# Position steps of a Fourier layer: turning tiles in halves of 64 rows, and where two splits stand

## The chip, the core and the metric

The kernel runs on one core of one Trainium2 chip. The metric is the device time of one execution in microseconds. The core has a matrix engine (TensorE, PE; its weight loads are shown as PEld), three engines for elementwise work (VectorE, DVE; ScalarE, ACT; GpSimd, POOL) and a queue engine (SyncE, SP). Each takes its instructions in a fixed order and waits on semaphores. Matmuls accumulate in PSUM, eight banks of 512 floats on each of 128 partitions; everything else lies in SBUF.

## The reference

Two layers over 2048 prompt rows and 512 sample rows of width 1024, in float32. The first is windowed attention; the change does not touch it. The second mixes by a two-dimensional Fourier transform over positions and over the channels of each of four groups, gates the result, projects it, adds the residual, and a last norm follows:

```python
def fourier_layer(x, g, w_gate, w_out):
    b, s, d = x.shape
    h = rmsnorm(x, g)
    hg = h.astype(jnp.float32).reshape(b, s, N_FGROUPS, FGROUP_CH)
    f = jnp.fft.fftn(hg, axes=(1, 3), norm="ortho").real
    f = f.reshape(b, s, d).astype(x.dtype)
    gate = h @ w_gate
    return x + (f * jax.nn.silu(gate)) @ w_out
...
return rmsnorm(x, final_norm)
```

## The kernel before

Float32 products are made of three matmuls: each operand is split into a high part, rounded to the matmul's input type (a cast on ScalarE), and a low part, the rest (a subtraction on VectorE), and `matmul3` (L91 to L94) adds high by high, high by low and low by high. So each operand costs one instruction on ScalarE and one on VectorE, and each block of a product three on TensorE.

The Fourier layer first transforms over channels, then over positions. The 2048 prompt positions are taken as 16 x 128: a radix-16 step by additions gives, for each of the frequencies k1 = 0 to 8, a real and an imaginary state (`gr`, `gs`, 128 x 1024), and `position` (L1363) multiplies these by cosine and sine tables. It works in two halves of 512 columns. For each half `halves_of` (L1349) splits the state, cosine products go into one bank (`A`), sine products into half of another (`B`), and from them four short VectorE instructions (L1391 to L1394) make rows of one or two tiles, `u` and its mirror (k1 and 16 - k1). Each tile is then multiplied by its gate, which was stored in DRAM as `s2d` (L1397).

A finished tile (128 positions x 1024 channels) is multiplied by the output weights `wo`. For that it has to be turned, channels onto partitions: eight transposes of 128 x 128 for a tile, four to a bank, on TensorE against an identity, then casts and subtractions out of PSUM into the two parts. The rows of a mirrored tile stand backwards, and are read backwards out of PSUM.

There are two ways from there.

- For the early frequencies (`step`, L1584, called from `emit` for 0 and 8, then 4, then 2), `split_T` (L993) turns each tile, and `finish` (L1417) multiplies it by all of `wo`, 24 matmuls of 512 columns into each of two banks `fo`, adds the residual, squares, takes the norm and writes the rows out. While TensorE works on these products, VectorE makes the states of the odd frequencies (L1706 to L1720).
- For frequencies 6, 1, 7, 3 and 5, `Outs` (L1430) takes both tiles of a pair together, and replaces the eight block products of the pair by seven (a Strassen scheme with sums of weights `T1`, `T2`, `T3`, `N4`, which were made earlier and stored). `operands` (L1470) turns the two tiles into four banks `tr` (L1442), makes the parts of the blocks themselves (`own`, L1446: cast L1449, subtraction L1450) and the sums of blocks `F1` to `F4` (`sums`, L1453: L1459, L1466) with their parts `S1` to `S4` (`split`, L986: cast L988, subtraction L990). `products` (L1483) issues seven products of twelve matmuls each into three banks `Wo`, `Zo`, `Xo`, and adds them to the residual tiles `xa`, `xb` (L1490).

The products of one pair and the position step of the next are interleaved by hand: `products` takes three hooks, and the loop at L1743 passes in `split_g` (loads and the first half's split), `transform` (the position step) and `turns` (operands of the next pair). In the steady steps TensorE thus does 84 matmuls of 512 columns, 12 of 260 (cosines), 12 of 256 (sines) and 16 transposes for each pair.

Within each engine a scheduler orders the instructions, from priorities in the order of recording and from dependences. `after(a, b)` (L134) pins one instruction behind another on its engine without a wait, and `seq(engine, ins)` (L139) pins it behind the last one that was given for the same key. The attention layer pins its long chains so; the Fourier layer pins only two sorts of instruction: the final scaling of a tile behind the last short instruction of a position step (`last_b`), and a few in the first products.

PSUM in this layer: three banks for the products (`psum2`), and five single banks in rotation (`psum3`, L1258) for the transposes and for `A` and `B`, all handed out by `bank` (L76). `left`, `right`, `xtile` and the tag `hT` (8 buffers) are pools of SBUF.

Of the kernel before, what the change touches and what calls it, by code (L numbers as in the profile page):

```python
# [9 lines left out]
F32 = mybir.dt.float32  # L10
# [9 lines left out]
P = 128  # L20
# [22 lines left out]
def encoder(  # L43
# [32 lines left out]
    def bank(name):  # L76
        return banks[-1].tile([P, 512], F32, tag="bank", name=name)

# [12 lines left out]
    def matmul3(out, a, b, start, stop, more=False):  # L91

        for i, j in ((0, 0), (0, 1), (1, 0)):
            pe(PE.matmul(out, a[i], b[j], start=start and i + j == 0, stop=stop and i == 1, skip_group_check=more))  # L94
# [871 lines left out]
    def fourier_phase(tail):  # L966
        with ExitStack() as es:
# [18 lines left out]
            def split(t, src, lo_engine=DVE):  # L986

                ACT.copy(t[:, 0], src)  # L988
                for cs in (slice(0, 256), slice(256, 512)) if lo_engine is POOL else (slice(0, 512),):
                    lo_engine.tensor_tensor(t[:, 1, cs], src[:, cs], f32(t[:, 0, cs]), ALU.subtract)  # L990
                return t[:, 0], t[:, 1]
# [20 lines left out]
            def sumsq(src, name, place=lambda ins: None):  # L1012
                ss = main.tile([P, 8], F32, tag="ss", bufs=2, name=f"ss{name}")
                junk = fp.tile([P, 512], F32, tag="c12", bufs=1, name=f"jk{name}").bitcast(BF16)
                ACT.activation(junk, src, AF.Square, accum_out=ss[:, 0:1])
                return inv_rms(ss, 1, f"inv{name}", place)
# [10 lines left out]
            class Pair:  # L1027
# [37 lines left out]
                def sums(self, i):  # L1065
# [4 lines left out]
                    if i % 2:  # L1070
# [3 lines left out]
                        2: lambda: (F[1], ps[0, 0], ALU.subtract),  # L1074
                        3: lambda: (ps[0, 0], out, ALU.subtract),
                        4: lambda: (ps[0, 1], F[2], ALU.subtract),
# [47 lines left out]
            def prod(out, a, b, ks, first):  # L1124

                for k in ks:
                    cs = slice(k * P, (k + 1) * P)
                    matmul3(out, (a[0][:, cs], a[1][:, cs]), b[k], first and k == 0, k == 3, not first)
# [129 lines left out]
            banks.append(es.enter_context(tc.tile_pool(name="psum3", bufs=5, space=PSUM, reuse_waits="tile")))  # L1258
# [76 lines left out]
            def gated(name, r, place):  # L1335
# [3 lines left out]
                if r[2] is None:  # L1339
                    SP.dma_start(s2, rows(src, (r[0] - off, r[1])))  # L1340
# [8 lines left out]
            def halves_of(name, gr, gs, hf):  # L1349

                out = []
                for i, g in enumerate((gr, gs)):
                    if g is not None:
# [3 lines left out]
                        DVE.tensor_tensor(t[:, 1], gv, f32(t[:, 0]), ALU.subtract)  # L1357
# [3 lines left out]
            last_b = [None]  # L1361

            def position(name, tab, gr, gs, tiles, loads=None, parts=None, between=None, later=None):  # L1363
# [3 lines left out]
                bp = bank(f"B{name}")  # L1367
                us = [zt(f"u{name}_{i}") for i in range(len(tiles))]
                for hf in range(2):
# [4 lines left out]
                    def acc(out, tabs, c0, n):  # L1374
                        for i, (w, t) in enumerate(zip(tabs, ts)):
# [4 lines left out]
                            matmul3(out, w, v, i == 0, i == len(ts) - 1)  # L1380

                    a = bank(f"A{name}_{hf}")[:, :260].rearrange("p (g c) -> p g c", g=2)
                    acc(a, (cs, ns), 0, 130)
                    b = bp[:, hf * 256 : hf * 256 + 256].rearrange("p (g c) -> p g c", g=2)
                    acc(b, (sn, cs), P, P)
# [9 lines left out]
                for u, s2 in zip(us, s2s):  # L1395
                    if later is None:
                        DVE.tensor_tensor(u, u, s2, ALU.mult)  # L1397
# [7 lines left out]

            def normed(x2, r):

                inv = sumsq(x2, f"f{r[0]}")
                after(DVE.scalar_tensor_tensor(x2, x2, inv[:, 0:1], gfb, ALU.mult, ALU.mult), last_b[0])
                SP.dma_start(out_rows(r), x2)  # L1410
# [6 lines left out]
            def finish(uT, r):  # L1417
                r0 = r[0]
                x2 = residual(r)
                for half in range(2):  # L1420
                    ps = psum2.tile([P, 512], F32, tag="acc", name=f"fo{r0}_{half}")
                    for k in range(KD):
                        matmul3(ps, uT[k], wo[half * KD + k], k == 0, k == KD - 1)
                    xs = x2[:, half * 512 : half * 512 + 512]
                    DVE.tensor_tensor(xs, xs, ps, ALU.add)
                normed(x2, r)
# [3 lines left out]
            class Outs:  # L1430
# [6 lines left out]
                def turn(self, i, hf):  # L1437
                    u, r = self.us[i]
                    ps = bank(f"tr{self.n}_{i}{hf}")
                    for k in range(4):  # L1440
                        c0 = (hf * 4 + k) * P
# [427 lines left out]
```

## Time and profile before

| what | value |
|---|---|
| time, median of 3 runs | 1581.89 us (1580.86 to 1582.9) |
| time of the profiled execution | 1581.36 us |
| its span, first to last instruction | 1579.4 us |
| granted TensorE clock, mean | 0.999 |
| ScalarE busy | 876.9 us (56%) |
| GpSimd busy | 446.1 us (28%) |
| HBM traffic | 236 GB/s over the span |

In rows of the profile a time stands first (us from the span's start), then a duration, the engine, the line of the kernel, the operation, output tile `<-` inputs with the numbers of buffers left out, the shapes, and how many such instructions in a row the line stands for. Matmuls overlap in the engine, so their durations (0.39 us for one of 512 columns) are longer than the distance between two of them. In brackets stands how long the engine had been idle before, and what ended that. "PEld" rows are the loads of the stationary operand, which can run under the matmul before.

### The profile page before, as it was taken

How to read it: one execution, taken by the hardware profiler on the slowest of the kernel's cores; microseconds unless marked ns; L12 is line 12 of the kernel's file. 1: busy time of each engine (PE TensorE's matmuls, PEld its weight loads, DVE VectorE, ACT ScalarE, POOL GpSimd, SP SyncE). 2: the span in 40 equal slices, each digit the busy share in tenths (PEclk: the TensorE clock that was granted, in tenths of full speed). 3: DMA queues.
4: the chain of work that ended last, by engine and by line, in shares of the span. 5: the costliest groups of instructions: out<-in, count | busy, mean ns of one | idle time of the engine just before them, and what ended most of it. 6: DMA issues, size and time to landing. Idle time of an engine off the chain costs nothing.

```text
span 1579.4 us, 27487 instructions
## 1 busy us (share of the span) xinstructions
PE 1569.1 (99%) x9754; PEld 1321.5 (84%) x9754; DVE 1152.7 (73%) x2793; ACT 876.9 (56%) x2096; POOL 446.1 (28%) x614
## 2 busy tenths in 40 slices
PE   9999999999999999999999999999999999999998
PEld 7888888888888888988888888888888888888886
DVE  6888656877547786378764577669878877989796
ACT  7788535776246784167752476646655554343242
POOL 2575642421404314024222242223112111010110
PEclk9999999999999999999999999999999999999999
DMA  8587695575856567665649556675557569557762
GB/s 302 200 332 283 226 360 210 207 257 202 295 209 222 204 235 272 223 208 220 257 161 334 211 212 227 246 251 204 203 202 259 177 219 407 181 182 299 280 208 80
DMA packets 100996, 373.89 MB, mean 237 GB/s; under 512 B 11267, under 2 KB 22283, under 8 KB 83452
## 3 DMA queue, kind: packets, MB, share of 16 engines
q1 hardware_dynamic: 83148, 298.17, 53.4%
q0 software_dynamic: 16400, 70.04, 11.5%
q10 hardware_dynamic: 1312, 3.94, 0.6%
q8 instruction: 77, 1.26, 0.3%
q14 instruction: 59, 0.48, 0.1%
HBM read 280.84 MB, written 91.26 MB: 236 GB/s over the span
## 4 chain that ended last, share of the span: by engine, by line
PE 95%; DVE 3%; DMA 1%; ACT 1%; issue 1%; POOL 0%; SPq 0%; POOLq 0%; ACTq 0%; DVEq 0%
PE gp L94 14%; PE qp L94 14%; PE spt L94 11%; PE op L94 7%; PE av L590 6%; PE W L94 6%; PE spt L505 6%; PE fo L94 5%; PE vp L94 3%; PE Wo L94 3%; PE Z L94 3%; PE pt L564 3%; PE z L94 2%; PE Zo L94 2%; PE X L94 2%; PE z L1112 1%
## 5 line engine op out<-in xcount | busy, mean ns | idle before, releaser
L94 PE MATMUL gp<-h,wg 128*128 128x512 f32 x960 | 237.8, 396 | 0.0
L94 PE MATMUL qp<-h,wq 128*128 128x512 f32 x960 | 236.9, 395 | 0.0
L524 DVE CUSTOM_DVE_ANT_0 S<-spt,b 128x385 f32<-128x385 f32 (+1 forms) x320 | 156.5, 527 | 105.2 <-PE spt L505 68.0
L94 PEld LDWEIGHTS gp<-h,wg 128*128 128x128 f32 x960 | 174.9, 188 | 37.3 <-issue 1.0
L94 PEld LDWEIGHTS qp<-h,wq 128*128 128x128 f32 x960 | 174.9, 188 | 36.3 <-issue 0.2
L532 ACT ACTIVATE S<-S 128x385 f32<-128x385 f32 (+1 forms) x320 | 188.8, 597 | 19.6 <-DVE S L524 19.3
L572 ACT CAST pts<-pt 128x384 fp32r<-128x384 f32 (+1 forms) x240 | 100.4, 458 | 165.6 <-PE pt L564 156.3
L573 DVE TENSOR_TENSOR pts<-pt,pts 128x384 fp32r<-128x384 f32 (+1 forms) x240 | 114.2, 519 | 23.9 <-ACT pts L572 22.9
L94 PE MATMUL spt<-wo,uT 128*128 128x512 f32 x480 | 120.4, 391 | 0.0
L614 POOL TENSOR_TENSOR uT<-o,uT 128x256 fp32r<-128x256 f32 x75 | 55.5, 740 | 229.6 <-ACT uT L613 224.9
L94 PE MATMUL op<-wo,uT 128*128 128x512 f32 x480 | 118.9, 391 | 0.0
L505 PE MATMUL spt<-kwin,qab 64*128 64x384 f32 (+1 forms) x960 | 118.9, 353 | 0.0
L590 PEld LDWEIGHTS av<-pts,v 128*128 128x128 f32 x576 | 101.4, 188 | 18.8
L94 PE MATMUL fo<-wo,tTu 128*128 128x512 f32 x480 | 115.8, 392 | 0.2 <-ACT wo L1624 0.2
L590 PE MATMUL av<-pts,v 128*128 128x512 f32 (+1 forms) x576 | 115.7, 341 | 0.0
L94 PEld LDWEIGHTS op<-wo,uT 128*128 128x128 f32 x480 | 89.3, 188 | 18.6
L94 PEld LDWEIGHTS spt<-wo,uT 128*128 128x128 f32 x480 | 89.1, 188 | 18.3
L94 PEld LDWEIGHTS fo<-wo,tTu 128*128 128x128 f32 x480 | 88.2, 188 | 17.5 <-ACT wo L1624 0.6
L544 DVE TENSOR_SCALAR S<-S 128x384 f32<-128x384 f32 (+1 forms) x192 | 95.8, 499 | 6.8
L505 PEld LDWEIGHTS spt<-kwin,qab 64*128 64x128 f32 x960 | 74.7, 186 | 28.3 <-issue 26.1
L610 POOL TENSOR_TENSOR o<-o,s 128x256 f32<-128x256 f32 x75 | 55.3, 737 | 134.9 <-DVE o L608 134.5
L564 PEld LDWEIGHTS pt<-ident,S 64*128 64x128 f32 x1328 | 78.4, 138 | 4.2 <-issue 2.1
(333 smaller groups left out, 3195.5 us busy)
## 6 DMA issues: line engine op xcount, KB each, us to landing
wo<-wsd SPq DMA_DIRECT2D x32, 1024.0 KB, 5.2
wq<-wsd SPq DMA_DIRECT2D x31, 1024.0 KB, 7.3
wg<-wsd SPq DMA_DIRECT2D x31, 1024.0 KB, 5.6
x<-x1d SPq DMA_DIRECT2D x40, 512.0 KB, 3.6
b<-b21d SPq DMA_DIRECT2D x40, 512.0 KB, 5.8
b<-rowd SPq DMA_DIRECT2D x40, 384.0 KB, 4.3
xs<-in_x_dram SPq DMA_DIRECT2D x23, 512.0 KB, 6.9
s2d<-gt POOLq DMA_DIRECT2D x40, 256.0 KB, 5.0
```

Source lines behind the costliest of these rows:

```text
L94: pe(PE.matmul(out, a[i], b[j], start=start and i + j == 0, stop=stop and i == 1, skip_group_check=more))
L505: pe(PE.matmul(banks[j][:, 2 + k0 * P : 2 + k1 * P], res["q"][rows, qp, b * P : (b + 1) * P], kwin[g][rows, kp, b * P + k0 * P : b * P + k ...
L524: seq(DVE, DVE.tensor_tensor_reduce(out=s[:, e0:e1], in0=ps[:, 1 + e0 : 1 + e1], in1=st["bias"][:, j, 386 - e1 : 386 - e0][:, ::-1], scale ...
L532: last_exp[0] = seq(ACT, ACT.activation(s[:, e0:e1], s[:, e0:e1], AF.Exp, bias=s[:, 386:387], scale=-1.0, accum_out=s[:, 387:388]))
L544: seq(DVE, DVE.tensor_scalar(s[:, ks], s[:, ks], den, None, ALU.mult))
L564: pe(PE.transpose(ps[h][:, kb, j, :], ss[j][rows, 1 + kb * P : 1 + (kb + 1) * P], ident[rows, rows]))
L572: seq(ACT, ACT.copy(hi, ps[:, k0:k1]))
L573: seq(DVE, DVE.tensor_tensor(lo, ps[:, k0:k1], f32(hi), ALU.subtract))
L590: pe(PE.matmul(to, v, pt, start=n == part == 0, stop=part == 1 and n in (1, len(todo) - 1), skip_group_check=n > 1,))
L610: eng.tensor_tensor(o, o, s, ALU.mult)
L614: low = eng.tensor_tensor(lo, o, f32(hi), ALU.subtract)
L1112: PE.matmul(to, m[part][:, g * P : (g + 1) * P], ch[:, 0, :, odd * P : (odd + 1) * P], start=part == 0, stop=part == 1,)
```

## The change

- **Turning.** From frequency 4 on, a tile is turned by 16 transposes of 64 rows x 128 columns in place of 8 of 128 x 128. The upper and the lower 64 rows go to two neighbouring banks, alternating (`half_turns`). Both tiles of a pair are turned one directly after the other, and pinned behind the matmuls that stand ahead of them. Whoever reads a turned block then reads pieces of 64, in turn from the two banks (`quarters`).
- **Banks.** The five single banks are given up after frequencies 0 and 8; in their place come two pairs of banks (`psum4`). Cosine and sine products of a half share one pair, and a turned tile takes one pair, so the two pairs rotate: first half, second half, first tile, second tile.
- **Order.** In `Outs` the parts of `S3` and of the last own block (`rest`) are recorded only in the next pair's first hook, behind the casts and low parts of the next position's first half; in the steady steps VectorE's and ScalarE's instructions of this stretch are pinned in that order by `seq`. The second half's split is recorded ahead of the position step. The old pair's last product and its norm are carried over into the next pair's first hook (`late`). `T3`'s product is issued as two halves of six matmuls, the turn between them.
- **Anchors.** On SP the reads of the gate and the writes of finished rows are pinned behind the last read of a state (`last_read`).

Matmuls with their shapes, casts, subtractions and DMAs are otherwise the same in number. In the built program of the steady step VectorE's order after the turn is: own part, three sums, two splits, fourth sum, add of `S3`'s product, final scale of `xa`, split of `S4`, own part, add of the old pair's `fN` product, add of the new pair's first product, low part, the norm's small instruction, low part, split of `S3`, last own part, final scale of `xb`, add of the `T1` product, two low parts. Before, the split of `S3` and the last own part stood directly ahead of the add of the `fN` product. TensorE's order after the turn is: 6 matmuls of the `T3` product, 12 of the new pair's first product, 7 of the `T1` product, 12 of the old pair's `fN` product, the other 5, one cosine matmul, 3 of the `T2` product, 3 cosine, 1 `T2`, 2 cosine and 6 sine matmuls, 8 `T2`, all 12 of the second half, then 12 `Zo`, 12 `Xo` and 6 `T3`. Before, 7 of `T3` stood behind the turn, and 2 of `T1` ahead of the `fN` product.

```diff
     def bank(name):
+        if turning:
+            return two_banks(name)[:, 0]
         return banks[-1].tile([P, 512], F32, tag="bank", name=name)
+    turning = []
+    def two_banks(name):
+        return turning[0].tile([P, 2, 512], F32, tag="two", name=name)
+    def half_turns(tiles):
+        views = []
+        for i, src in enumerate(tiles):
+            two = two_banks(f"tw{i}")
+            views.append(two.rearrange("p h (k q) -> p k h q", k=KD))
+            for k in range(KD):
+                for h in range(2):
+                    hp = slice(64 * h, 64 * h + 64)
+                    ins = PE.transpose(two[:, h, 64 * k : 64 * k + 64], src[hp, k * P : (k + 1) * P], ident[hp, hp])
+                    after(seq("turns", ins), chain["B"])
+        return views
+    def quarters(t):
+        return t.rearrange("p (k h q) -> p k h q", k=4, h=2)
...
+                    if turning:
+                        ab = two_banks(f"AB{name}_{hf}")
+                        a, b = ab[:, 0, :260], ab[:, 1, :256]
+                    else:
+                        a, b = bank(f"A{name}_{hf}")[:, :260], bp[:, hf * 256 : hf * 256 + 256]
...
                 def operands(self):
-                    self.turn(0, 0)
+                    self.turns()
                     self.own(0, 0)
-                    self.turn(1, 0)
-                    self.turn(1, 1)
-                    self.sums(1)
-                    self.sums(2)
-                    self.turn(0, 1)
+                    for i in (1, 2, 3):
+                        self.sums(i)
+                    self.halve(1)
+                    self.halve(2)
                     self.sums(4)
+                def others(self):
+                    self.halve(4)
                     self.own(0, 1)
-                    self.sums(3)
+                def rest(self):
+                    self.halve(3)
                     self.own(1, 1)
...
+                    chain["turns"] = prod(W, S[3], ft["T3"], (0, 1), False)
                     hooks[2]()
+                    def upper():
+                        prod(W, S[3], ft["T3"], (2, 3), False, chain["turns"])
+                        seq("dve", add(xb, 1, W))
...
                     if not last:
                         prod(W, A[1, 1], ft["N4"], four, False)
-                        add(xb, 0, W)
-                        normed(xb, self.us[1][1])
-                        return
+                        seq("dve", add(xb, 0, W))
+                        return xb, self.us[1][1]
...
+            p3.close()
+            turning.append(es.enter_context(tc.tile_pool(name="psum4", bufs=2, space=PSUM, reuse_waits="tile")))
             emit(4)
...
-                    nxt["p"] = [halves_of(name, *gl, 0), None]
+                    scaled = []
+                    def weigh():
+                        if late[0]:
+                            scaled.append(norm(*late[0], "dve"))
+                    nxt["p"] = [halves_of(name, *gl, 0, weigh), None]
+                    o.rest()
+                    for f in scaled:
+                        f()
...
+                    nxt["p"][1] = halves_of(name, *gl, 1)
                     nxt["o"] = Outs(k1, position(name, k1, *gl, tiles, (nxt["s"], tb), nxt["p"], third))
```

More of the change, by code (lines that the diff above doesn't have):

```diff
@@ L89, in inv_rms, with matmul3 @@
         return inv
[L91 removed]
+    def matmul3(out, a, b, start, stop, more=False, behind=None):
         for i, j in ((0, 0), (0, 1), (1, 0)):
[L94 removed]
+            ins = pe(PE.matmul(out, a[i], b[j], start=start and i + j == 0, stop=stop and i == 1, skip_group_check=more))
+            after(ins, behind)
+        return ins
     def fetch_w(n, name, late=None):
@@ L1586, in step @@
                 if pend:
-                    finish(*pend.pop(0))
-                new = [(split_T(u, f"u{r[0]}", r[2] is not None), r) for u, r in new]
+                    end = finish(*pend.pop(0))
+                if turning:
+                    chain["turns"] = end
+                    new = turned(new)
+                else:
+                    new = [(split_T(u, f"u{r[0]}", r[2] is not None), r) for u, r in new]
                 for f in pend:
```

173 lines of the change are left out of this document (111 added, 62 removed).

## The prediction

> **What bounds the kernel now.** I read the page's first part and its chain of waits, then the busy time by stretch over the end of the run, then the instructions in order of time.
>
> ```profile
> span 1579.4 us, 27487 instructions
> PE 1569.1 (99%) x9754; PEld 1321.5 (84%) x9754; DVE 1152.7 (73%) x2793; ACT 876.9 (56%) x2096; POOL 446.1 (28%) x614
> ...
> PE 95%; DVE 3%; DMA 1%; ACT 1%; issue 1%; POOL 0%; SPq 0%; POOLq 0%; ACTq 0%; DVEq 0%
> ```
>
> TensorE is busy 99% of the span and holds 95% of the chain, so a microsecond taken from its queue is a microsecond of time unless TensorE then waits. The change touches only the end, from the position step of frequency 4 (1376 us) on. By stretch (columns: busy us and instructions of TensorE, weight loads, VectorE, ScalarE, GpSimd, then clock and DMA):
>
> ```profile
> 1391.00:1418.00 27.00, 26.75 (x137) 22.43 (x136) 26.25 (x37) 12.15 (x21) 2.84 (x3) 1.00 0.43 144
> 1418.00:1449.10 31.10, 30.79 (x153) 25.74 (x152) 29.04 (x40) 8.66 (x18) 1.43 (x2) 1.00 0.63 235
> ...
> 1475.00:1499.10 24.10, 24.10 (x126) 20.45 (x125) 21.15 (x37) 10.07 (x21) 4.05 (x4) 1.00 0.70 246
> ```
>
> TensorE is full in the third row, which is one steady step, and VectorE is 88% busy beside it (21.15 of 24.10). Around the steps of frequencies 2 and 6 VectorE is fuller still (26.25 of 27.00, 29.04 of 31.10). The steady step on TensorE, in order of time:
>
> ```profile
> 1462.70 0.90 PE L94 MATMUL Ap<-gp,tbp 128*128 128x260 f32 x6
> 1463.43 0.87 PE L94 MATMUL Bp<-gp,tbp 128*128 128x256 f32 x6
> 1464.14 2.91 PE L94 MATMUL Wo<-fT,S 128*128 128x512 f32 x12
> ...
> 1473.85 1.30 PE L94 MATMUL Wo<-fT,S 128*128 128x512 f32 x5
> 1474.98 1.91 PE L1442 MATMUL tr<-ident,up 128*128 128x128 f32 x16
> 1476.65 1.86 PE L94 MATMUL Wo<-fT,S 128*128 128x512 f32 x7
> 1478.35 2.88 PE L94 MATMUL Wo<-wo,tT 128*128 128x512 f32 x12
> ...
> 1481.53 2.89 PE L94 MATMUL Wo<-fN,tT 128*128 128x512 f32 x12
> 1484.26 2.43 PE L94 MATMUL Zo<-fT,S 128*128 128x512 f32 x10
> ...
> 1490.83 1.06 PE L94 MATMUL Ap<-gp,tbp 128*128 128x260 f32 x6
> 1491.73 2.03 PE L94 MATMUL Zo<-wo,S 128*128 128x512 f32 x8
> ...
> 1499.09 1.91 PE L1442 MATMUL tr<-ident,up 128*128 128x128 f32 x16
> ```
>
> From one turn (L1442) to the next are 1499.09 - 1474.98 = 24.11 us. A 512-wide matmul takes 0.227 us (12 from 1481.53 to 1484.26), a cosine half 0.122 (6 from 1462.70 to 1463.43), a sine half 0.118 (6 to 1464.14). The old turn: 1473.85 to 1478.35 is 4.50 us for 5 + 7 matmuls and 16 transposes; less 12 x 0.227 = 2.72 the turn costs 1.78. The step holds 84 wide matmuls, 12 cosine and 12 sine ones: 19.07 + 1.46 + 1.42 + 1.78 = 23.73 us. The other 0.38 are waits, such as the six cosine matmuls at 1490.83, which take 0.90 instead of 0.73.
>
> **The change, part by part.** *The turns.* Seven turns of two tiles (frequencies 4, 2, 6, 1, 7, 3, 5) go from 16 transposes of 128x128 to 32 of 64x128, in pairs on two row halves. The attention stage holds this very shape:
>
> ```profile
> 389.07 4.27 PE L94 MATMUL spt<-wo,uT 128*128 128x512 f32 x18
> 393.27 0.64 PE L564 MATMUL pt<-ident,S 64*128 64x64 f32 x13
> 393.70 0.22 PE L564 MATMUL spt<-ident,S 64*128 64x64 f32 x1
> ...
> 394.01 0.22 PE L564 MATMUL spt<-ident,S 64*128 64x64 f32 x1
> 394.16 4.39 PE L94 MATMUL spt<-wo,uT 128*128 128x512 f32 x18
> 398.39 1.54 PE L590 MATMUL av<-pts,v 128*128 128x512 f32 x8
> ```
>
> From 389.07 to 398.39 are 9.32 us for 36 wide matmuls (8.17) and 24 half transposes: 1.15 us. The pairs follow at (394.01 - 393.70) / 5 = 0.062, so 12 pairs are 0.74 and 0.41 is left over. The weight loads show what that is:
>
> ```profile
> 393.27 0.51 PEld L564 LDWEIGHTS pt<-ident,S 64*128 64x128 f32 x13 [0.35 <-issue]
> ```
>
> ```profile
> 1474.85 1.80 PEld L1442 LDWEIGHTS tr<-ident,up 128*128 128x128 f32 x16
> ```
>
> The first half-height weight load starts at 393.27, with its own transpose and after 0.35 us without a load; the full-height one at 1474.85 runs 0.13 ahead of its transpose, under the matmul before. Going over to half height and back costs 0.41. One turn becomes 16 x 0.062 + 0.41 = 1.40 us: 0.38 saved, 2.7 over seven. Bounds: 0.99 if going over cost nothing here, 1.78 if nothing is gained; I take 1.40, since shape, banks and neighbours are those of the attention rows.
>
> The Trainium skill, TensorEngine Tiling (Array Packing), section Overview, gives up to twofold speed for a small dimension of 64 or less; its section Tiling Modes adds that changing the mode drains the engine. The trace sides with the second: by twofold speed alone a turn would be 0.89 us, and the seven 3.6 us less than in my sum.
>
> *The order on VectorE.* In the steady step S3's split and the last own split (L990, L1450) go behind the lower parts of the next position's first half (L1357). VectorE now:
>
> ```profile
> 1467.09 0.69 DVE L1490 TENSOR_TENSOR x<-x,Wo 128x512 f32<-128x512 f32 x1 [1.53 <-PE Wo L94]
> ...
> 1483.27 0.68 DVE L1450 TENSOR_TENSOR tT<-tr,tT 128x512 fp32r<-128x512 f32 x1
> 1483.87 0.68 DVE L990 TENSOR_TENSOR S<-F,S 128x512 fp32r<-128x512 f32 x1
> 1484.47 0.68 DVE L1450 TENSOR_TENSOR tT<-tr,tT 128x512 fp32r<-128x512 f32 x1
> 1485.07 1.27 DVE L1490 TENSOR_TENSOR x<-x,Wo 128x512 f32<-128x512 f32 x2
> 1486.26 0.68 DVE L1357 TENSOR_TENSOR gp<-go,gp 128x512 fp32r<-128x512 f32 x1
> ...
> 1487.09 0.68 DVE L1357 TENSOR_TENSOR gp<-go,gp 128x512 fp32r<-128x512 f32 x1
> 1487.33 0.87 POOL L88 TENSOR_TENSOR invf<-invf,mhalf 128x1 f32<-128x1 f32 x1 [3.70 <-DVE invf L87]
> 1488.23 1.29 DVE L1409 SCALAR_TENSOR_TENSOR x<-x,invf,gfb 128x1024 f32<-128x1024 f32 x1 [0.46 <-POOL invf L88]
> ...
> 1489.43 0.68 DVE L1490 TENSOR_TENSOR x<-x,Zo 128x512 f32<-128x512 f32 x1
> 1490.03 1.29 DVE L1357 TENSOR_TENSOR gp<-go,gp 128x512 fp32r<-128x512 f32 x2
> ```
>
> A split moves the next start by 0.60. Today VectorE reaches the add of the old tile's last product (`Wo<-fN`, 1485.07) late: that product ended at 1481.53 + 2.89 = 1484.42. Without the two splits ahead VectorE is there at 1483.87, 8.89 us after the turn's start. But in the new order the product stands 6 + 12 + 7 + 12 = 37 matmuls behind the turn, not 33: it is issued by 1.40 + 37 x 0.227 = 9.80 and ends 0.17 later, and VectorE follows 0.04 after (1467.09 against 1464.14 + 2.91), at 10.01. The order is fixed, so all behind that add waits 1.1 us although the lower parts have their inputs. From its start I read off the rows: second add ends +1.28 (0.60 + 0.68), first lower part ends +1.87, second +2.70; then the two splits (1.20, new here) and the 1024-wide scale at +3.82 (POOL's power ended at +3.13, so its wait goes), then the third lower part (+5.62) ends +6.30, the fourth +6.91.
>
> TensorE meanwhile, with 0.05 from VectorE to TensorE: five Zo to 10.93, one cosine matmul to 11.06; the next product reuses the bank that the second add reads and waits to 11.34 (0.28); three wide and three cosine matmuls and a wide one to 12.61; the second lower part is there at 12.76 (0.15); two cosine, six sine, eight wide to 15.53; one cosine to 15.65, third lower part 16.36 (0.71), three cosine to 16.73, fourth lower part 16.97 (0.24). New waits: 1.38 a step, in place of 0.38.
>
> So a step is 19.07 + 2.88 + 1.40 + 1.38 = 24.73 instead of 24.11: +0.62, three times (positions 7, 3, 5 under the products of 1, 7, 3): +1.9. Bounds of these waits: 0.38, if they come out as today, and 1.9, if each of the four also shows the 0.13 of a weight load.
>
> *The other four turns* (4, 2, 6 and 5, under no such step) save 0.38 each: -1.5. For 4 and 2 this needs VectorE, which is nearly full there, to keep up; were the two swallowed, 0.8 would be lost. The last step keeps one bank wait behind the second add: +0.2.
>
> *At nothing.* The shared pair of banks: the second half's pair is free once the last own split has read it (+3.22 + 0.68, at 13.9), and its first matmul comes at 15.5; without these 1.6 us it would be a fifth wait. The delayed splits feed products more than 5 us on. In the steady steps SP's queue keeps its order, and GpSimd's table load only trades places with a power that now has 0.7 us to spare. Before the step of frequency 2, one load of odd sums goes behind an output write. ScalarE already waits for the loads there:
>
> ```profile
> 1389.52 1.06 ACT L1704 ACTIVATE tm<-od 128x1024 f32<-128x1024 f32 x1 [10.50 <-DMA od<-odd]
> ```
>
> It waits for a later one, whose place stays; VectorE behind it is nearly full, so each microsecond that this load came later would be one of time. I take nothing.
>
> Sum: 1.9 - 1.5 + 0.2 = +0.5 or so. The profiled execution took 1581.36 around its span of 1579.4, which gives 1581.9; it lies 0.5 below the median of the three runs (1581.89), from which it is 1582.4. I say **1582.2**.
>
> **The rivals** (times from the median). *Going over is free here* (the drain is hidden): turns at 0.99 save 7 x 0.79 = 5.5 instead of 2.7, so -2.3: 1579.6. Against it stands the load at 393.27. The twofold figure of the Trainium skill's page TensorEngine Tiling (Array Packing), section Overview, would lead here too.
>
> *The waits on VectorE don't come*: steps keep at most today's 0.38, three times 1.0 less and the last wait gone: -2.7, 1579.2; with waits fully gone, 1.1 more, 1578.1. For it: VectorE is ahead of the add by 1.1 us. Against it: the add is in front of the lower parts on one engine, and its product's end is set by TensorE.
>
> *Slower: reading turned tiles costs more.* Each evacuation now walks two banks in pieces of 64, alternating. Pieces of 64 out of one bank cost nothing extra:
>
> ```profile
> L572 ACT CAST pts<-pt x240: 372/480/501, 48.2 to 1024.4; 128x384 fp32r<-128x384 f32 x96, 128x256 fp32r<-128x256 f32 x24
> ```
>
> ```profile
> L1449 ACT CAST tT<-tr 128x512 fp32r<-128x512 f32 x15 | 8.8, 585 | 30.1 <-PE tr L1442 30.1
> ```
>
> (480 ns for 384 columns, 585 for 512, 0.82 a column), but no row shows alternating banks. At 1.3 times, seven VectorE reads a step grow by 0.2. In a steady step the spare 1.1 us takes up six of them almost; ScalarE's first and the seventh show: 0.5, three times. In the full stretches four reads for each turn of 4 and 2 show, 0.8 each, and 6 and 1 some 0.5 each: +4.1, so +4.6: 1586.5. It decides once a read costs about 1.25 times.
>
> *The change doesn't do what it says*: the halves don't overlap, 32 x 0.062 + 0.41 = 2.4 a turn, +7.5: 1589.4. The attention rows speak against it.
>
> **How the numbers follow.** Forecast 0.58, free going-over 0.09, no waits 0.11, slow reads 0.18, no overlap 0.04. The runs shown spread 2 us; 0.2%, 3.2 us, is about what a measurement can tell from no change. Faster by that (under 1578.7) takes the lower part of the no-waits case and a little of the free one: 0.10. Slower (over 1585.1) takes most of slow reads, no overlap and a margin of the forecast for a full VectorE: 0.24. Within: 0.66. The range, from no waits at all to slow reads, is 1578.3 to 1586.6; the forecast's own is 1580.7 to 1584.
>
> **What would show it.** The half transposes in a turn start 0.12 late behind a 0.35 gap in weight loads, and 32 take some 1.4 us. From turn to turn the steps of 7, 3 and 5 take 24.7. VectorE idles about 1 us before the add of the `fN` product, and the second half's cosine matmuls wait for lower parts. Wrong: a step under 24.1, VectorE reads of the turned tiles well over 0.68, or turns near 1.0.

## The result and the profile after

The changed kernel takes 1584.05 us (median of 16 runs, 1582.48 to 1586.2) where the kernel before, on the same chip, takes 1581.37 (16 runs, 1579.92 to 1583.69): ratio 1.0016, 95% interval 1.0009 to 1.0022. That is 2.7 us more, inside the 0.2% named as no change. The forecast, 1582.2 us, was 0.3 above the median of the three runs known then (1581.89); its sum of parts was +0.5.

The page after, its span, busy times and chain of waits:

```profile
span 1581.7 us, 27701 instructions
PE 1567.9 (99%) x9866; PEld 1316.5 (83%) x9866; DVE 1151.6 (73%) x2793; ACT 878.3 (56%) x2096; POOL 443.1 (28%) x614
...
PE 91%; DVE 4%; DMA 2%; ACT 1%; issue 1%; POOL 0%; SPq 0%; ACTq 0%; POOLq 0%; DVEq 0%
```

TensorE issues 112 matmuls more and is busy 1.2 us less (1567.9 against 1569.1), yet the span is 2.3 us longer: its share of the chain falls from 95% to 91%, VectorE's rises from 3% to 4% and DMA's from 1% to 2%. The end of the run, cut at the starts of the turns of frequencies 4, 2, 6, 1 and 7 (columns as in the prediction's table by stretch), first of the kernel before:

```profile
1390.38:1417.48 27.10, 26.84 (x137) 22.54 (x136) 26.14 (x36) 12.35 (x22) 2.84 (x3) 1.00 0.45 151
1417.48:1449.14 31.66, 31.35 (x158) 26.29 (x157) 29.60 (x41) 8.66 (x18) 1.43 (x2) 1.00 0.63 234
1449.14:1474.98 25.84, 25.84 (x134) 22.05 (x134) 20.77 (x36) 9.10 (x19) 3.59 (x5) 1.00 0.99 383
1474.98:1499.09 24.11, 24.11 (x125) 20.46 (x125) 21.16 (x37) 10.07 (x21) 4.05 (x4) 1.00 0.70 246
```

and of the changed kernel, with one step more:

```profile
1389.36:1415.96 26.60, 26.35 (x154) 21.84 (x154) 25.32 (x36) 12.91 (x22) 2.84 (x3) 1.00 0.44 159
1415.96:1448.57 32.61, 31.94 (x179) 26.22 (x178) 30.95 (x42) 8.86 (x18) 3.06 (x4) 1.00 0.61 229
1448.57:1474.96 26.39, 25.23 (x148) 20.82 (x148) 20.67 (x35) 9.02 (x19) 3.79 (x4) 1.00 0.98 361
1474.96:1500.38 25.42, 24.44 (x142) 19.69 (x142) 21.16 (x36) 10.19 (x21) 3.01 (x4) 1.00 0.71 265
1500.38:1525.18 24.80, 24.26 (x142) 19.68 (x142) 21.17 (x36) 10.19 (x21) 3.04 (x4) 1.00 0.54 187
```

The granted clock is 1.00 in every row. In the steady steps (fourth row before, fourth and fifth after) TensorE was busy all the time; now it is idle for 0.5 to 1.0 us that the rows show, and waits some more inside groups. The third row holds the most idle time, 1.16 us. The first row is shorter by 0.50, the second longer by 0.95.

The rows do not all hold the same work, for the turns also moved in TensorE's queue. The turn of 6, with which the third row starts, has 28 products of the tile before behind it in the kernel before, and 24 in the changed one:

```profile
1450.80 6.62 PE L94 MATMUL fo<-wo,tTu 128*128 128x512 f32 x28
```

```profile
1449.70 5.74 PE L117 MATMUL fo<-wo,tTu 128*128 128x512 f32 x24
```

Counted in TensorE's rows, the second row has 116 wide matmuls before and 120 after, the third 93 and 90 (one more stands ahead of the turn at its end), the first 96 and a steady step 84 in both, and the rest behind the turn of 5 has one less. At 0.227 us each that is +0.91, -0.68 and -0.23 us of work that only changed its stretch.

Runs differ by up to 2 us in when the first turn starts (1389.4 to 1391.5 among the profiles of the changed kernel and its variants, which have the same work ahead of it), so profiles are compared here from turn to turn. From the first turn to the end of the span are 1579.4 - 1390.38 = 189.0 us before and 1581.7 - 1389.36 = 192.3 after.

The turn itself, TensorE after, in order of time:

```profile
1499.83 0.61 PE L117 MATMUL Wo<-fT,S 128*128 128x512 f32 x2
1500.38 1.21 PE L95 MATMUL tw<-ident,up 64*128 64x64 f32 x32
1501.51 1.66 PE L117 MATMUL Wo<-fT,S 128*128 128x512 f32 x6
1503.01 2.89 PE L117 MATMUL Wo<-wo,tT 128*128 128x512 f32 x12
```

From 1499.83 to 1503.01 are 3.18 us for eight wide matmuls (8 x 0.227 = 1.82) and the turn: 1.36 us, where 1.40 was forecast and 1.78 was paid before. The weight loads pause for 0.35 us ahead of the first half transpose here too, as in the attention rows. What follows it on VectorE, in order of time in the same step:

```profile
1501.75 0.69 DVE L1524 TENSOR_TENSOR tT<-tw,tT 128x512 fp32r<-128x512 f32 x1 [1.94 <-ACT tT L1523]
1502.36 1.40 DVE L1541 TENSOR_TENSOR F<-F,tw 128x512 f32<-128x512 f32 x2
...
1508.80 0.68 DVE L1524 TENSOR_TENSOR tT<-tw,tT 128x512 fp32r<-128x512 f32 x1
1510.24 1.29 DVE L1572 TENSOR_TENSOR x<-x,Wo 128x512 f32<-128x512 f32 x2 [0.75 <-PE Wo L117]
1511.44 0.68 DVE L1404 TENSOR_TENSOR gp<-go,gp 128x512 fp32r<-128x512 f32 x1
...
1512.86 0.69 DVE L1015 TENSOR_TENSOR S<-F,S 128x512 fp32r<-128x512 f32 x1
1513.46 0.69 DVE L1524 TENSOR_TENSOR tT<-tw,tT 128x512 fp32r<-128x512 f32 x1
...
1515.86 1.29 DVE L1404 TENSOR_TENSOR gp<-go,gp 128x512 fp32r<-128x512 f32 x2
```

and on TensorE:

```profile
1511.17 0.28 PE L117 MATMUL ABp<-gp,tbp 128*128 128x260 f32 x1
1511.58 0.97 PE L117 MATMUL Wo<-fT,S 128*128 128x512 f32 x3
...
1515.91 0.28 PE L117 MATMUL ABp<-gp,tbp 128*128 128x260 f32 x1
1516.60 1.83 PE L117 MATMUL ABp<-gp,tbp 128*128 128x260 f32 x11 [0.41 <-DVE gp L1404]
1518.27 2.90 PE L117 MATMUL Zo<-wo,S 128*128 128x512 f32 x12
```

VectorE takes 0.68 to 0.69 us for its reads of the turned tiles (L1524 here, 0.70 for the pair at L1541), as before. It then stands idle for 0.75 us until TensorE has the product with the last weights, and everything pinned behind that addition (1510.24) comes late. TensorE shows it in two places: the sum's product starts at 1511.58, where the one cosine matmul before it was through at 1511.17 + 0.12 = 1511.29; and between 1515.91 and 1518.27 twelve matmuls of the second half, 1.44 us of work, take 2.36.

The wait for the residual read in the changed kernel, on VectorE in order of time:

```profile
1460.78 0.69 DVE L1572 TENSOR_TENSOR x<-x,Wo 128x512 f32<-128x512 f32 x1 [3.57 <-DMA x<-x1d]
1461.38 0.68 DVE L1404 TENSOR_TENSOR gp<-g1r,gp 128x512 fp32r<-128x512 f32 x1
...
1462.05 0.68 DVE L1404 TENSOR_TENSOR gp<-g1s,gp 128x512 fp32r<-128x512 f32 x1
```

on TensorE behind it:

```profile
1462.12 1.89 PE L117 MATMUL ABp<-gp,tbp 128*128 128x260 f32 x11 [1.12 <-DVE invf L110]
```

and VectorE at the same place before:

```profile
1459.03 0.68 DVE L1357 TENSOR_TENSOR gp<-g1r,gp 128x512 fp32r<-128x512 f32 x1
1459.63 0.68 DVE L1357 TENSOR_TENSOR gp<-g1s,gp 128x512 fp32r<-128x512 f32 x1
...
1462.48 0.69 DVE L1490 TENSOR_TENSOR x<-x,Wo 128x512 f32<-128x512 f32 x1 [1.50 <-DMA x<-x1d]
```

Both kernels wait there for the rows of `x1d`. Before, the two lower parts of the first half (L1357, 1459.03 and 1459.63) stood ahead of the waiting addition, and TensorE never saw the wait: its work in that stretch, 93 wide matmuls, 24 of the position step and a turn, is 25.77 us of 25.84. Now the addition (1460.78) stands ahead of them (1461.38, 1462.05), and TensorE idles for 1.12 us at 1462.12, just after the first of them is done (1461.38 + 0.68 = 1462.06). The row names the small instruction right behind it.

### The profile page after: what moved, and what is told of

Read it like the earlier page. It is cut to its first block, busy times and chain, and to the rows that moved or that the text cites. A ratio compares the mean times of both kernels' runs of the same rounds, so it can differ in the third digit from the quotient of the medians.

```text
span 1581.7 us, 27701 instructions
## 1 busy us (share of the span) xinstructions
PE 1567.9 (99%) x9866; PEld 1316.5 (83%) x9866; DVE 1151.6 (73%) x2793; ACT 878.3 (56%) x2096; POOL 443.1 (28%) x614
## 4 chain that ended last, share of the span: by engine, by line
PE 91%; DVE 4%; DMA 2%; ACT 1%; issue 1%; POOL 0%; SPq 0%; ACTq 0%; POOLq 0%; DVEq 0%
PE gp L117 14%; PE qp L117 14%; PE spt L117 11%; PE op L117 7%; PE W L117 6%; PE av L615 6%; PE spt L530 6%; PE vp L117 3%; PE Z L117 3%; PE fo L117 3%; PE pt L589 3%; PE Wo L117 2%; PE z L117 2%; PE X L117 2%; PE Zo L117 1%; PE z L1153 1%
```

## The experiments

The first five runs take the changed kernel and undo or move one thing in each.

**Full turns in the changed order.** Sixteen transposes of 128x128 again, into the same pairs of banks. The readers go back to pieces of 128 columns out of one bank each.

```diff
-                for h in range(2):
-                    hp = slice(64 * h, 64 * h + 64)
-                    ins = PE.transpose(two[:, h, 64 * k : 64 * k + 64], src[hp, k * P : (k + 1) * P], ident[hp, hp])
+                out = two[:, k // 4, (k % 4) * P : (k % 4) * P + P]
+                ins = PE.transpose(out, src[:, k * P : (k + 1) * P], ident)
```

> The changed kernel with one edit: each of the seven turns transposes in 16 full tiles of 128 rows again, into the same pairs of banks; order, banks and pinning stay. Theory (the half tiles themselves pay, 0.38 to 0.42 us for each turn, and the lost time comes from the order behind them): each turn takes 1.78 us instead of 1.36 to 1.40, so the kernel is about 7 x 0.4 = 2.8 us longer than the changed one: 1586 to 1588 us where the kernel before takes 1581.4, and every reader of a turned tile on VectorE keeps 0.68 to 0.70 us. Rival (the half tiles give nothing on the whole path, since what follows them waits for other work or reads more slowly): no more than 1 us longer than the changed kernel, 1584 to 1585 us, or even shorter.

Measured: 1585.38 us (9 runs), 1.3 more than the changed kernel and 1.0027 of the kernel before (1.0017 to 1.0037). That is between the 1584 to 1585 us of the rival and the 1586 to 1588 us of the theory. Its first two stretches and one steady step:

```profile
1391.46:1417.95 26.49, 26.49 (x138) 22.61 (x137) 25.11 (x35) 12.82 (x22) 2.84 (x3) 1.00 0.46 159
1417.95:1450.53 32.58, 32.24 (x161) 27.03 (x160) 30.59 (x42) 8.86 (x18) 2.62 (x4) 1.00 0.63 233
...
1502.48:1527.68 25.20, 24.66 (x126) 20.40 (x124) 21.25 (x36) 10.28 (x21) 3.03 (x4) 1.00 0.56 183
```

The step is 25.20 against 24.80, the 0.4 of a turn. The first two stretches are 26.49 and 32.58 against 26.60 and 32.61: there the longer turn costs nothing. What gives it back is a wait of TensorE for a lower part in the second stretch, first of the changed kernel in order of time:

```profile
1436.48 0.65 PE L117 MATMUL ABp<-gp,tbp 128*128 128x260 f32 x3 [0.67 <-DVE gp L1404]
```

and of this one:

```profile
1438.86 0.63 PE L116 MATMUL ABp<-gp,tbp 128*128 128x260 f32 x3 [0.34 <-DVE gp L1403]
```

0.67 us shrink to 0.34. In the first stretch the changed kernel waits 0.25 us for a lower part at 1403.70, and this one does not wait at all: its work there is 26.45 of 26.49 us. With the shorter turn TensorE arrives earlier and waits longer for VectorE, which is busy 25.11 of 26.49 and 30.59 of 32.58 us. The third stretch, with the wait for the residual, doesn't gain either: 26.20 here, 26.39 with half turns. So the half turn pays in the steps and behind the last turn (32.21 here, 31.72 with half turns), and not in the three stretches from the turn of frequency 4 to that of 1.

**Both splits ahead.** The order of the two splits as it was, all else as changed.

```diff
                 def others(self):
                     self.halve(4)
                     self.own(0, 1)
-
-                def rest(self):
                     self.halve(3)
                     self.own(1, 1)
+
+                def rest(self):
+                    pass
```

> The changed kernel with the two splits (of the third sum and of the last own quarter) back ahead of the lower parts; half turns, paired banks and pinning stay. Theory (the waits of each steady step come from VectorE's fixed order, the pinned additions and the two splits between lower parts): the three steps fall from 24.8 to about 24.1 to 24.3 us, the stretch of 26.4 us ahead of them stays, and the time falls by 1.5 to 2.1 us to about 1582.2 us. Rival (the two rotating pairs of banks, or the additions pinned ahead, make the waits, whatever the splits do): steps stay within 0.2 us of 24.8 and the time stays at 1584 us. A second rival (the splits ahead keep the later weight or sum reads waiting as they did in the kernel before): steps grow, 1585 us or more.

Measured: 1582.68 us (11 runs; 1.0007 of before, 0.9998 to 1.0016), steps of 24.48 to 24.50. A gain of 1.4 us and of 0.3 in a steady step: less than the theory's, more than the rival's.

**The third sum's split ahead alone.** `self.halve(3)` moves from `rest` to the end of `others`; the last own split stays behind.

> The changed kernel with only the split of the third sum back ahead of the lower parts; the split of the last own quarter, which is the last reader of the turned tile and so sets when its pair of banks comes free, stays behind them. Theory (VectorE's order makes the waits): about 0.5 to 0.7 us less in each of the three steps, 24.1 to 24.3 us, and 1582.0 to 1582.6 us in all, as good as with both splits ahead. Rival (the banks' release makes the waits): as the release is as late as in the changed kernel, steps stay at 24.8 us and the time at 1584 us, and only the kernel with both splits ahead gains.

Measured: 1581.99 us (11 runs; 1.0003, 0.9994 to 1.0012), steps of 24.19 to 24.22, as the theory had it, and better than with both ahead. VectorE around the pinned addition, in order of time, with one split ahead:

```profile
1509.64 0.68 DVE L1015 TENSOR_TENSOR S<-F,S 128x512 fp32r<-128x512 f32 x1
1510.48 1.28 DVE L1572 TENSOR_TENSOR x<-x,Wo 128x512 f32<-128x512 f32 x2 [0.15 <-PE Wo L117]
...
1515.49 1.28 DVE L1404 TENSOR_TENSOR gp<-go,gp 128x512 fp32r<-128x512 f32 x2
```

and with both, from the run before this one:

```profile
1510.18 0.68 DVE L1524 TENSOR_TENSOR tT<-tw,tT 128x512 fp32r<-128x512 f32 x1
1510.78 1.27 DVE L1573 TENSOR_TENSOR x<-x,Wo 128x512 f32<-128x512 f32 x2
...
1515.72 1.28 DVE L1404 TENSOR_TENSOR gp<-go,gp 128x512 fp32r<-128x512 f32 x2
```

One split (1509.64) fits into the 0.75 us of idle time: 0.15 are left, and the addition starts when the product is there. The second (1510.18) does not fit: the addition no longer waits for TensorE but for VectorE's own queue, and comes 0.37 us later than in the changed kernel, counted from the turns (at 1500.55 with both, at 1500.62 with one, at 1500.38 in the changed kernel). VectorE also waits 0.45 us for GpSimd there, ahead of the scaling.

What a step takes follows the second half's first lower part (the last rows above, and 1515.86 in the changed kernel). It ends 16.16 us behind the turn in the changed kernel, 15.85 with both splits ahead and 15.55 with one; the steps are 24.80, 24.50 and 24.20.

**The last own split ahead alone**, `self.own(1, 1)` moved in the same way.

> The changed kernel with only the split of the last own quarter back ahead of the lower parts; the third sum's split stays behind them. Theory (VectorE has room for one split, and not for two, in the time in which it waits for the product with the last weights, so which of the two goes ahead is all the same): steps of 24.2 us as with the third sum's split alone ahead, and 1581.6 to 1582.4 us. Rival (it is the third sum's split whose place matters, or the pair of banks that the last own quarter holds): steps of 24.5 us or more, as with both ahead or as in the changed kernel, and 1582.6 us or more.

Measured: 1581.5 us (11 runs; 0.9999, 0.999 to 1.0008), steps of 24.20 to 24.22. Which of the two fills the gap is all the same. It also settles the banks: the last own split, which frees the pair of banks, ends 9.7 us behind the turn here, 13.2 with the other split ahead and 13.8 in the changed kernel. The first two have the same steps, so the release does not set them.

**The residual's reads first.** In the step of frequency 6 the loads for the second sum go behind them on SP.

```diff
-            f_sums("T2", right)
             finish(*pend.pop(0))
             finish(*pend.pop(0), o.operands)
             o.others()
             o.load()
+            f_sums("T2", right)
```

> The changed kernel with one edit: in the first position step the two loads for the sums behind the turned tiles are issued behind the reads of the residual rows instead of ahead of them; nothing on the compute engines is moved. Theory (the addition pinned ahead of the lower parts waits 3.6 us for the residual rows there, and TensorE behind it for the lower parts): the stretch between the third and fourth turns falls from 26.4 to 24.8 to 25.2 us, VectorE's first addition there no longer names the read of the residual, and the time falls by 1.2 to 1.6 us to about 1582.6 us. Rival (the stretch is long for its other waits, for the squares and the tables, and the read is hidden behind them): it stays over 26 us and the time at 1584 us. The loads that go behind could come late instead: then the products of the sums wait for them and the time is the same or longer.

Measured: 1581.67 us (11 runs; 1.0004, 0.9995 to 1.0013), 2.4 less than the changed kernel. TensorE at the same place, in order of time:

```profile
1460.76 1.61 PE L117 MATMUL ABp<-gp,tbp 128*128 128x260 f32 x12
```

and the busy times of this stretch and the next:

```profile
1448.60:1473.32 24.72, 24.72 (x148) 20.78 (x148) 20.76 (x35) 9.02 (x19) 3.79 (x4) 1.00 1.04 409
1473.32:1498.12 24.80, 24.26 (x141) 19.69 (x140) 21.17 (x36) 10.20 (x21) 3.01 (x4) 1.00 0.69 247
```

Twelve matmuls run through without a hole, and the stretch is 24.72 instead of 26.39: 1.67 less, a little more than the 1.2 to 1.6 expected. The other 0.6 are in the step behind it, 24.80 instead of 25.42. ScalarE in that step of the changed kernel:

```profile
1482.98 1.28 ACT L1403 CAST gp<-go 128x512 fp32r<-128x512 f32 x2 [1.08 <-DMA go<-god]
```

A read of the next state landed 1.08 us late for the casts. ScalarE's square behind them was late too, and VectorE waited 0.69 us for it (at 1487.39) ahead of its second lower part. With the residual's reads first this wait isn't there, and the step is like the other two. But it is not there either in the three runs that move a split and leave the reads as they were (first steps of 24.48, 24.22 and 24.22), while it is there, 0.96 us, with full turns. So the late read goes with the 0.6 us; that the order of the residual's reads makes it late is not shown.

**Both edits together**: the third sum's split ahead, the residual's reads first.

> The changed kernel with the third sum's split ahead and with the residual's reads issued ahead of the loads for the sums. Theory (two separate losses, each in its own stretch): 24.7 us from the third turn to the fourth and 24.2 us for each of the three steps, so 1584.05 - 1.7 - 0.6 x 3 - 0.6 = about 1580.0 us, 1.5 us under the kernel before. Rival (one and the same loss, removed twice, or the reads that go earlier collide with others): 1581.5 us or more, no better than either edit alone.

Measured: 1581.15 us (11 runs; 0.9999, 0.999 to 1.0008). The stretches are as expected, 24.72 and three times 24.20, and from the first turn to the end are 1579.5 - 1391.21 = 188.3 us, 1.7 less than with the reads alone. The time, between the theory's 1580.0 and the rival's 1581.5, is only 0.5 less than with the reads alone; in its profile 1.8 us of that stand ahead of the first turn (1391.21 against 1389.42), in work that both kernels share. Of that I know no cause.

**The scaling behind the second half's lower parts**, on top of both.

```diff
                     o.rest()
-                    for f in scaled:
-                        f()
+                    nxt["scaled"] = scaled
...
                     nxt["p"][1] = halves_of(name, *gl, 1)
+                    for f in nxt["scaled"]:
+                        f()
```

> The kernel with both of these edits, and the scaling of the old pair's second row tile recorded behind the second half's lower parts instead of ahead of them, so that they stand 1.2 us earlier in VectorE's order. Theory (the last wait left in a step is the one for these lower parts): steps fall from 24.2 to 23.7 to 23.9 us, and the time by another 0.9 to 1.5 us to 1578.5 to 1579.1 us. Rival (the scaling only moves: its output, its buffer or the additions behind it come 1.2 us late and hold the next products as long): steps of 24.1 us or more and 1579.8 us or more.

Measured: 1578.85 us (11 runs; 0.9987, 0.9978 to 0.9996), steps of 23.88 to 23.89. The wait at the second half is gone: its twelve matmuls take 1.44 us (1512.69 to 1514.13), and nothing on TensorE waits behind the scaling.

**Full turns in this order**: the edit of the first experiment on top of the last kernel.

> The same kernel without that last edit, and with full turns of 128 rows in place of the half tiles. Theory (where TensorE is not held by VectorE's order, a half turn saves its 0.4 us whole, and in the two first stretches, which VectorE fills, nothing): steps and the stretch from the third turn to the fourth grow by 0.4 us each, 24.3 and 25.1 us, the first two stretches stay at 26.5 and 32.6 us, and the time is 1.9 to 2.1 us more than with half turns, 1580.6 to 1581.0 us. Rival (the half tiles are hidden here too): no more than 0.8 us more.

Measured: 1581.3 us (11 runs; 1.0 of before, 0.9991 to 1.0009), 2.45 more than with half turns, a little above the 1.9 to 2.1 expected. Stretches of 26.48, 32.60, 25.11, then steps of 24.29 to 24.30: four times 0.4 more, and from the first turn to the end 189.3 against 187.2 us, 2.1 more. So the half turns give 2.1 us in this order and 1.3 in the changed one, and in both nothing in the first two stretches.

**The first half's lower parts ahead of the pinned addition**, on top of the kernel with the scaling behind:

```diff
-                    nxt["p"] = [halves_of(name, *gl, 0, weigh), None]
+                    nxt["p"] = [nxt["first"], None]
+                    weigh()
...
+                def ahead():
+                    nxt["o"].others()
+                    if k2:
+                        nxt["first"] = halves_of(f"p{k2}", *nxt["r"][0], 0)
```

> The kernel with the split ahead, the residual's reads first and the scaling behind, and with the two lower parts of the next position's first half moved ahead of the pinned addition of the last product in VectorE's order. Theory (this addition, which waits for TensorE's product with the last weights, is what is left in front of the first half's lower parts): steps fall from 23.9 to 23.4 to 23.7 us, and the time by 0.5 to 1.2 us to 1577.7 to 1578.4 us. Rival (what the two lower parts gain, the addition itself and the second one behind it lose, since the sum's product waits for them): steps stay at 23.8 to 24.0 us and the time at 1578.5 to 1579.2 us.

Measured: 1577.42 us (11 runs; 0.9978, 0.9969 to 0.9987): by the medians 4.1 us less than the kernel before, by the ratio 3.5, and a little better than the theory's numbers. TensorE in a step, in order of time:

```profile
1508.36 1.60 PE L117 MATMUL ABp<-gp,tbp 128*128 128x260 f32 x12
1509.80 2.94 PE L117 MATMUL Wo<-fT,S 128*128 128x512 f32 x12
```

and the busy times of the step ahead of it:

```profile
1474.17:1497.56 23.39, 23.39 (x141) 19.67 (x140) 20.98 (x36) 10.18 (x21) 2.69 (x4) 1.00 0.70 236
```

The twelve matmuls of the first half now run as one group (1508.36 to 1509.80), where the changed kernel has them in three. The step's work by the prediction's prices is 19.07 + 2.88 + 1.36 = 23.31 us; it takes 23.39. No wait of any size is left in it.

**The late splits alone, in the kernel before.**

```diff
                     self.sums(3)
-                    self.own(1, 1)
...
                     nxt["p"] = [halves_of(name, *gl, 0), None]
+                    o.rest()
```

(`rest` holds the two splits, as in the changed kernel.)

> The kernel before, full turns, single banks and no pinned order, with one part of the change alone: the splits of the third sum and of the last own quarter go behind the lower parts of the first half. Theory (the late splits cost only because the change also pins the addition of the last product ahead of the lower parts): steps stay at 24.0 to 24.2 us and the time at 1580.9 to 1581.9 us. Rival (splits behind the lower parts cost wherever they are, since the second half's lower parts then wait for them): steps of 24.5 to 24.8 us and 1582.9 to 1583.8 us.

Measured: 1580.69 us (11 runs; 0.9996, 0.9987 to 1.0005), steps of 24.00, 23.81 and 23.78 against 24.11, 24.08 and 24.07: the late splits cost nothing here, as the theory has it, and even gain a little, which it had not. VectorE there:

```profile
1508.03 1.28 DVE L1498 TENSOR_TENSOR x<-x,Wo 128x512 f32<-128x512 f32 x2
1509.23 1.29 DVE L1357 TENSOR_TENSOR gp<-go,gp 128x512 fp32r<-128x512 f32 x2
1510.43 0.69 DVE L990 TENSOR_TENSOR S<-F,S 128x512 fp32r<-128x512 f32 x1
```

The additions find their products done (no idle time ahead of 1508.03), the lower parts (1509.23) follow at once and the splits stand behind them. Moving the splits gains 0.1 to 0.3 a step here; in the changed kernel, where the addition waits for its product, having them behind costs 0.3 against both ahead (24.80 and 24.50) and 0.6 against one.

## Why the prediction was right, and where it was not

Where the 3.3 us from the first turn to the end came from, beside what the working had put there. The third column is the work that only changed its stretch, at 0.227 us a wide matmul; the last is what is left without it:

| part | forecast | measured | moved work | without it |
|---|---|---|---|---|
| turns of 4 and 2, with their stretches (58.76 to 59.21) | -0.8 | +0.45 | +0.91 | -0.46 |
| turn of 6 and its stretch (25.84 to 26.39) | -0.4 | +0.55 | -0.68 | +1.23 |
| three steps (72.26 to 75.02) | +1.9 | +2.76 | 0 | +2.76 |
| from the last turn to the end (32.16 to 31.72) | -0.2 | -0.44 | -0.23 | -0.21 |

*The price of a turn* was right: 1.36 against 1.40. The going over to half height cost 1.36 - 16 x 0.062 = 0.37 here. The attention rows carried it, and the rival of a free going-over (0.99) falls. The Trainium skill, TensorEngine Tiling (Array Packing), section Tiling Modes, says that a change of mode drains the engine, without a time for it. The 0.37 us fit that; no run here shows what the engine does in them. The twofold speed that the Trainium skill's same page, section Overview, gives as the most is not reached: 1.78 to 1.36 is 1.3-fold.

*The order on VectorE* was right, by place and by size. The addition was put at 10.01 us behind the turn's start and came at 9.86; the bank wait at 0.28 is 0.29 (1511.29 to 1511.58); the third lower part was to end at 16.31 and ended at 16.16. The waits sum to 24.80 - 23.31 = 1.49 where 1.38 was worked out: 0.29 at the bank, 0.92 at the second half's two lower parts (0.71 + 0.24 forecast), and 0.28 in small gaps, where 0.15 for the first half's second lower part had been put. Steps of 24.80 stand against 24.73. The runs that move a split show the cause: the second half's lower part comes late behind an addition that waits 0.75 us for its product and behind two splits, and step and lower part move by the same 0.3 and 0.6 us. The rival that the waits don't come falls with the steps, and "slow reads" with VectorE's 0.68 to 0.70 us a read.

*The step that failed is the saving at the other four turns (4, 2, 6 and 5), put at 0.38 each, -1.5.* With the +0.2 of a bank wait that made -1.3; without the moved work it came to +0.56. For 5 it held (-0.21). For 4 and 2 the working named the condition, that VectorE keeps up, and what its failing would lose, 0.8; both runs with full turns show that it fails (26.49 and 26.48, 32.58 and 32.60 there, against 26.60 and 32.61 with half turns). The -0.46 of these two stretches are not the turns' doing, since with full turns in the new order they are as short. I took the saving all the same, though the quoted rows had VectorE at 26.25 of 27.00 and 29.04 of 31.10. For 6 the working left out a wait: the pinned order puts the first addition ahead of the lower parts there too, and that addition waits for a DMA. The run that puts the residual's reads first takes 1.67 us off this stretch, and then the half turn's 0.4 show in it (24.71 against 25.11 with full turns). The trace of before held this wait, 1.50 us on VectorE at 1462.48, where it cost nothing because of what stood ahead of it; the working looked for TensorE's products behind the pinned additions and not for their other operand.

*A term missing from the first steady step*: 0.6 us, with the late read of the state. "SP's queue keeps its order" had put the DMA side of these steps at nothing.

*How far it was luck.* The forecast of no change held, and the way (slower) was right. But the sum was +0.5 where 2.7 us were measured (3.3 from the first turn), a difference clear of the noise and close to the 3.2 named as the limit. The measured 1584.05 lies just above the forecast's own range (1580.7 to 1584), and well inside the whole one only because that reached up to slow reads, which didn't come. That parts missed by 2.8 us in all still fitted into the band for no change is luck. The ends of the range, 1578.3 and 1586.6, are also not quite those of the rivals' sums, 1578.1 and 1586.5.

*What stays open.* Why the read of the state is late in some of these kernels. What shortens the first two stretches by some 0.5 us in the new order. That VectorE's order swallows the half turns of 4 and 2 is read from its waits and busy times; no run took work from it there. The anchors on SP were not moved alone. Nor was it tried whether the scatter ahead of the first turn can be had shorter.

## What to carry to other kernels

When an order is pinned on a busy engine, look at every operand of each pinned instruction, DMAs too, and at what stands ready behind it: a wait that was harmless ahead of other work becomes a wait of the engine that sets the end. A saving on the bounding engine is worth its size only in the stretches where no other engine fills the time; read that from the busy times by stretch before multiplying it by the number of places. A gap ahead of a pinned instruction holds just the work that fits: here one split of 0.6 us in 0.75, and with two the additions behind come late. Before two stretches are compared, count the work in them: a turn that had moved by four matmuls in its queue looked like 0.9 us of lost time.

## What was unexpected

With 32 transposes of 64 rows in one go, the 0.37 us for going over and back are still a quarter of the turn's 1.36 us. Reads that alternate between two banks in pieces of 64 columns took no longer than reads of one bank (0.69 and 0.68 us). And the work ahead of the first turn, the same in all variants of the changed kernel, ended at 1389.4 to 1391.5 us in their profiles: as large a spread as what most of the edits gave.
